# The second MLP of a two-layer encoder: the norm's scale and bias, applied to x at one place or in eight parts

## The chip, the core and the metric

The kernel runs on one core of one Trainium2 chip. The metric is the device time of one execution in microseconds (us): 1342.46 us before the change. The engines are PE (TensorE, matmuls; PEld are its weight loads), DVE (VectorE), ACT (ScalarE), POOL (GpSimd) and SP (SyncE, which issues most DMAs). Each runs its own list of instructions in order and waits for others through semaphores.

## What is computed

A trunk of two layers, 512 tokens of 1024 float32 features. Each layer is a token mixer (gated DeltaNet in layer 0, gated linear attention, GLA, in layer 1) and a squared-ReLU MLP, and each of these ends in a residual sum and a LayerNorm:

```python
x = _layernorm(DEEPNORM_ALPHA * x + m, ln1_g[i], ln1_b[i])           # m: the mixer
a = jax.nn.relu(jnp.matmul(x, mlp_w1[i]))                            # 1024 -> 4096
x = _layernorm(DEEPNORM_ALPHA * x + jnp.matmul(a * a, mlp_w2[i]),    # 4096 -> 1024
               ln2_g[i], ln2_b[i])
```

The change lies between the second `ln1` and the second MLP.

## The kernel before

**x twice.** After the GLA mixer, x exists in two forms. The transposed form, `xth` and `xtl` (a rounded high part and the rest), is what the first matmul of the MLP reads; its scale and bias were applied while it was copied out of PSUM (L168). The row form, `xt[t]` for the four tiles t of 128 tokens, each in two halves of 512 columns, is what the residual needs. When the MLP starts, it has only been centred and divided by its deviation (`whiten`, L198); scale and bias still have to be applied to it. `affine` (L200) does this: a multiplication by g (L203) and an addition of b (L204) for each half, DVE instructions on 128x512 float32. Over four tiles these are sixteen instructions, eight of each kind. g and b are broadcast to 128 partitions by four DMAs (`load_ln`, L225) into two tiles of `ln_tile`.

**The MLP.** `mlp` (L333) has 32 blocks of 128 features, in four groups of eight. The first group is computed plainly: four blocks in `proj_halves`, then f = 4 to 7 one by one in `feature`. The other three groups are computed by a seven-product scheme of the Strassen kind: `pairs` makes two blocks at a time from products 1, 2, 5, 6, 7, 3, 4 (in this order) of sums of weight halves and of sums of x. The sums of x are made once, by `combos` (L389), a generator that is advanced step by step while f = 3 to 7 run; each operand is a pair, high (ACT, L398) and low (DVE, L399). Of these, operand 3 is the last of `t_pair(2)`, and operand 7 is written over a part of x after feature 7. The second matmul uses the same scheme over 512-wide products, in `seconds`: 21 products m = 0 to 20 of four units u each, every unit six matmuls; results are added to `xt` by `adds` (L534 the first time, L536 after that).

**Order.** The loop at L758 alternates one step of `pairs` with one unit of `seconds`; in this text, product 3 means the first pair's unless another is named. All matrix products are split: high x high, high x low, low x high (`mm3`, L114), so each operand needs a cast on ACT and a subtraction on DVE (`split`, L88). Before anything runs, the framework fixes each engine's order: among the instructions that its own model of time holds ready, it takes the one that was traced first, except those marked urgent, which go ahead. Three orders are prescribed: PE's and POOL's from L723 on, and ACT's inside the loop (L757), as traced. DVE's isn't prescribed. DVE therefore takes later-traced work whenever it expects nothing earlier to be ready.

**Memory.** A tile with a tag shares its slots with others of that tag, and a new one waits until every instruction that reads or writes the old one is done, those traced later too. Two lines matter:

```python
tiles = [pool.tile([P, 2, 512], F32, name=f"ln{i}", tag=f"t{4 + i}", bufs=1) for i in range(2)]
return tuple(pool.tile([P, HF, HT], F32R, name=f"t{2 * i + j}", tag=f"t{2 * i + j}", bufs=1) for j in range(2))
```

The first is `ln_tile` (L539): g lies in tag t4, b in t5. The second is `t_pair` (L384): `t_pair(2)`, operand 3, has the tags t4 and t5 too, with one slot each.

In `combos` before, the four calls of `affine` stand between operand 6 and the sum for operand 3. Traced, they come with f = 4 (t = 0), f = 5 (t = 1, 2) and f = 6 (t = 3).

Of the kernel before, what the change touches and what calls it, by code (L numbers as in the profile page):

```python
# [13 lines left out]
ALU = mybir.AluOpType  # L14
# [7 lines left out]
NT = S // P  # L22
# [6 lines left out]
class Ctx:  # L29
# [167 lines left out]
        for q in range(2):  # L197
            nc.scalar.activation(xs[q], xs[q], AF.Identity, scale=rstd[:, 0:1], bias=nmr[:, 0:1])  # L198

    def affine(self, t, par):  # L200

        for q, x in enumerate(self.xh(t)):
            self.nc.vector.tensor_tensor(x, x, par[q], ALU.mult)  # L203
            self.nc.vector.tensor_tensor(x, x, par[2 + q], ALU.add)  # L204

    def rsqrt(self, out, x, n, scale, eps):

# [125 lines left out]
def mlp(c, w1, w2, g, b, left, before=None, out=None):  # L333
# [13 lines left out]
    with c.banks(pj=2, X=2, Y=2, Z=2), tc.tile_pool(name="mlp", bufs=2) as pool:  # L347
        acts, par, lnp = [], [], []
# [34 lines left out]
        def t_pair(i):  # L383
            return tuple(pool.tile([P, HF, HT], F32R, name=f"t{2 * i + j}", tag=f"t{2 * i + j}", bufs=1) for j in range(2))  # L384

        def x_block(i, j):
            return tuple(t[:, HF * j:HF * j + HF, HT * i:HT * i + HT] for t in (c.xth, c.xtl))

        def combos():  # L389

            f = lambda t: t.bitcast(F32)
            tmp = pool.tile([P, 2, HF, HT], F32, name="tx", tag="h", bufs=3)
            u, v = tmp[:, 0], tmp[:, 1]
            a12, a21, a22 = x_block(0, 1), x_block(1, 0), x_block(1, 1)
            op = {1: x_block(0, 0), 2: a12, 4: a22}

            def pair_of(i, src, dst):
                A.copy(dst[0], src)  # L398
                V.tensor_tensor(dst[1], src, f(dst[0]), ALU.subtract)  # L399
                op[i] = dst  # L400

            def diff(out, a, b):
                V.tensor_tensor(out, f(a[0]), f(b[0]), ALU.subtract)
                V.tensor_tensor(out, out, f(a[1]), ALU.add)
                V.tensor_tensor(out, out, f(b[1]), ALU.subtract)

            def neg(out, a, b):
                V.scalar_tensor_tensor(out, a, -1.0, f(b[0]), ALU.mult, ALU.subtract)
                V.tensor_tensor(out, out, f(b[1]), ALU.subtract)

            diff(v, a22, a21)
            yield op
            pair_of(5, v, t_pair(0))
            yield op
            diff(u, op[1], a21)
            yield op
            neg(v, u, a22)
            yield op
            pair_of(6, v, t_pair(1))
            yield op  # L420
            if before:
                for t in range(NT):
                    c.affine(t, lnp)
                    yield op
            neg(v, v, a12)
            yield op
            pair_of(3, v, t_pair(2))
            yield op
            while not_done:
                yield op  # L430
            pair_of(7, u, a21)

        def urgent():
            return tc.high_priority()
# [91 lines left out]
        def pair(src, where="ah"):  # L526
            return c.split(src, [P, HF, HT], pool=ring(where))

        def add(t, hf, ps, op=ALU.add, cs=slice(0, 512)):
            xs = c.xh(t)[hf][:, cs]  # L530
            ps = ps[:, cs]
            if (t, hf) not in touched:
                touched.add((t, hf))
                V.scalar_tensor_tensor(xs, xs, ALPHA, ps, ALU.mult, op)  # L534
            else:
                V.tensor_tensor(xs, xs, ps, op)  # L536
# [5 lines left out]
        def quarters(h):  # L542
            return [h[j][:, :, HT * i:HT * i + HT] for i in range(2) for j in range(2)]
# [4 lines left out]
        def split_q(gi, i, q):  # L548

            parts.setdefault((gi, i), []).append(c.split(blocks[BLOCK[i] + (q,)], [P, 2, 512], pool=ring("w2")))  # L550
            if (gi, i) != (0, 1):
                sums(i, q)
            if i in (6, 7, 3, 4):
                load_part(gi + 1, *BLOCK[i], q)

        def sums(i, q):

            for x, y in PLUS.get(i, ()):
                a, b = blocks[x + (q,)], blocks[y + (q,)]
                if i == 5:  # L560
                    V.tensor_tensor(a, a, b, ALU.add)
                else:
                    nc.gpsimd.dma_start(a, b, accum_op=ALU.add)  # L563

        def seconds(hs, tail):

            seq = [(gi, i) for gi in range(G - 1) for i in (1, 2, 5, 6, 7, 3, 4)]
            left = {}

            def operand(gi, i):  # L570
                a11, a12, a21, a22 = quarters(hs[gi])
                if i == 5:
                    V.tensor_tensor(a11, a11, a21, ALU.subtract)
                    V.tensor_tensor(a21, a22, a21, ALU.subtract)
                if i == 6:
                    V.scalar_tensor_tensor(a21, a11, -1.0, a22, ALU.mult, ALU.subtract)
                    V.scalar_tensor_tensor(a12, a12, -1.0, a21, ALU.mult, ALU.subtract)
                left[gi, i] = pair({1: a11, 2: a12, 5: a21, 6: a21, 7: a11, 3: a12, 4: a22}[i])

            def banks(tag):  # L580
                return [c.bank([P, 512], F32, name="p" + tag, tag=tag) for _ in range(2)]

            def adds(i, j, ps):
                if i in (1, 2):
                    add(j, 0, ps)
                elif i in (5, 7):
                    add(2 + j, 1, ps, ALU.subtract)
                else:
                    add(j, 1, ps, ALU.subtract) if i in (6, 3) else add(2 + j, 0, ps)

            for q in range(2):
                split_q(0, 1, q)
            operand(0, 1)
            yield
            due = []
            for m, (gi, i) in enumerate(seq):
                nx = seq[m + 1] if m + 1 < len(seq) else None
                if i == 1:
                    X, Y = banks("X"), banks("Y")
                Z = None if m == 0 else Z  # L600
                if m == 1:
                    Z = banks("Z")
                bk = {2: Z, 5: Y, 3: Y}.get(i) or X
                for u in range(4):
                    q, j = divmod(u, 2)
                    wh, wl = parts[gi, i][q]
                    ah, al = left[gi, i]
                    sl = slice(j * P, (j + 1) * P)
                    for k in (2 * q, 2 * q + 1):
                        c.mm3(bk[j], ah[:, k, sl], al[:, k, sl], wh[:, k % 2, :], wl[:, k % 2, :],  # L610
                              (i in (1, 5) or m == 1) and k == 0, k == HF - 1, skip_group_check=True)
                    with urgent():
                        for d in due:
                            adds(*d)
                    due = [(i, j, bk[j])] if q and (i != 2 or gi == G - 2) else []
                    if i in (6, 4) and u == 2:
                        with urgent():
                            adds(*due.pop())
                    if m == 0 and u < 2:
                        sums(1, u)  # L620
                    if nx:
                        if u in (0, 2):
                            split_q(*nx, u // 2)
                        elif u == 1:
                            operand(*nx)
                    if m >= len(seq) - 2:
                        next(tail, None)
                    yield
            for d in due:
                adds(*d)  # L630
# [92 lines left out]
        with c.in_order(mybir.EngineType.PE), c.in_order(mybir.EngineType.Pool):  # L723
            hs = {0: h}
            tail = last(G - 1, hs)
            units = seconds(hs, tail)
            halves = c.proj_halves(specs, between)
            for f, ps in enumerate(halves):
                done = act(ps, h[0][:, f, :])
                load_part(0, 0, f // 2, f % 2, done if f > 1 else None)  # L730
                if f == 0 and before:
                    lnp.extend(c.load_ln(*before, ln_tile(), acts[0]))
                    c.cols = None
            combo = combos()
            def run(n):
                for _ in range(n):
                    next(combo, None)
            op = next(combo)
# [1051 lines left out]
```

## Time and profile before

| | |
|---|---|
| time, median of 3 runs | 1342.46 us (1341.44 to 1342.73) |
| span of the profiled execution, first to last instruction | 1340.6 us |
| second MLP's loop of `pairs` and `seconds`, about | 1051 to 1290 us of the span |
| `affine`, first and last start | 1032.3 and 1045.9 us |

The execution that was profiled has no time of its own beside its span; the median is 1.9 us longer, which is what lies around the first and the last instruction. In the timeline's rows, the first number is the start in us from the span's start, the second the duration; then engine, line, operation, output<-inputs, shape and count. Instructions of one engine overlap a little: the next one starts before the one ahead has ended, so a step from start to start says what an instruction costs its engine. A bracket at the end of a row gives the idle time ahead of it and who ended it. In the table of windows, the columns are busy us and counts of PE, PEld, DVE, ACT and POOL, then the granted PE clock (1.00 is full), the DMA share and GB/s.

### The profile page before, as it was taken

How to read it: one execution, taken by the hardware profiler on the slowest of the kernel's cores; microseconds unless marked ns; L12 is line 12 of the kernel's file. 1: busy time of each engine (PE TensorE's matmuls, PEld its weight loads, DVE VectorE, ACT ScalarE, POOL GpSimd, SP SyncE). 2: the span in 40 equal slices, each digit the busy share in tenths (PEclk: the TensorE clock that was granted, in tenths of full speed). 3: DMA queues.
4: the chain of work that ended last, by engine and by line, in shares of the span. 5: the costliest groups of instructions: out<-in, count | busy, mean ns of one | idle time of the engine just before them, and what ended most of it. 6: DMA issues, size and time to landing. Idle time of an engine off the chain costs nothing.

```text
span 1340.6 us, 22226 instructions
## 1 busy us (share of the span) xinstructions
PE 1324.5 (99%) x8802; PEld 1141.1 (85%) x8802; DVE 1103.2 (82%) x1738; ACT 757.4 (56%) x1445; POOL 98.9 (7%) x160
## 2 busy tenths in 40 slices
PE   9999999999999999999999999999999999999997
PEld 7778887888888899999998988888889899999986
DVE  6798898998768888988977687977777998889885
ACT  4766657666534656656663354654467566566640
POOL 6700000000001000101001000000000000001000
PEclk9999999999999999999999999999999999999999
DMA  6321111211133665556430422222225766556411
GB/s 179 80 64 49 48 48 48 64 46 46 53 112 109 197 133 157 125 159 166 118 95 32 122 85 63 64 64 64 84 74 146 185 171 145 126 165 132 142 65 48
DMA packets 152248, 136.47 MB, mean 102 GB/s; under 512 B 9025, under 2 KB 123745, under 8 KB 152144
## 3 DMA queue, kind: packets, MB, share of 16 engines
q1 hardware_dynamic: 145280, 111.62, 28.3%
q0 software_dynamic: 6720, 23.16, 8.9%
q8 instruction: 69, 1.13, 0.4%
q14 instruction: 35, 0.29, 0.1%
q10 hardware_dynamic: 144, 0.26, 0.1%
HBM read 114.06 MB, written 2.10 MB: 87 GB/s over the span
## 4 chain that ended last, share of the span: by engine, by line
PE 86%; DVE 6%; ACT 5%; issue 1%; DMA 1%; DVEq 0%; ACTq 0%
PE pq L120 6%; PE pq L119 6%; PE pq L117 6%; PE pX L119 3%; PE pX L120 3%; PE pX L117 3%; PE pjv L117 3%; PE pjv L120 3%; PE pjv L119 3%; PE pl L119 2%; PE pl L117 2%; PE pl L120 2%; PE scp L1015 2%; PE op L1720 2%; PE lv L1583 2%; PE pY L119 2%
## 5 line engine op out<-in xcount | busy, mean ns | idle before, releaser
L98 ACT CAST wh<-wst 128x1024 fp32r<-128x1024 f32 (+1 forms) x179 | 177.4, 994 | 158.0 <-DVE wst L448 52.8
L99 DVE TENSOR_TENSOR wl<-wst,wh 128x1024 fp32r<-128x1024 f32 (+1 forms) x179 | 205.6, 1151 | 43.5 <-ACT wh L98 43.1
L99 DVE TENSOR_TENSOR w2l<-w2r,w2h 128x1024 fp32r<-128x1024 f32 x84 | 102.5, 1220 | 23.1 <-ACT w2h L98 23.1
L120 PE MATMUL pq<-xth,wl 128*128 128x256 f32 x384 | 108.6, 283 | 0.0
L117 PE MATMUL pq<-xth,wh 128*128 128x256 f32 x384 | 108.5, 283 | 0.0
L119 PE MATMUL pq<-xtl,wh 128*128 128x256 f32 x384 | 108.5, 283 | 0.0
L98 ACT CAST w2h<-w2r 128x1024 fp32r<-128x1024 f32 x84 | 88.1, 1049 | 4.6 <-DMA w2r<-in_mlp_w 2.2
L120 PE MATMUL pq<-t,wl 128*128 128x256 f32 x288 | 81.4, 282 | 0.6 <-DVE wl L99 0.6
L117 PE MATMUL pq<-t,wh 128*128 128x256 f32 x288 | 81.0, 281 | 0.1
L119 PE MATMUL pq<-t,wh 128*128 128x256 f32 x288 | 81.1, 281 | 0.0
L119 PEld LDWEIGHTS pq<-xtl,wh 128*128 128x128 f32 x384 | 73.4, 191 | 3.0
L117 PEld LDWEIGHTS pq<-xth,wh 128*128 128x128 f32 x384 | 73.3, 191 | 2.9
L119 PE MATMUL pX<-w2l,ah 128*128 128x512 f32 x192 | 75.5, 393 | 0.0
L120 PE MATMUL pX<-w2h,al 128*128 128x512 f32 x192 | 75.4, 393 | 0.0
L117 PE MATMUL pX<-w2h,ah 128*128 128x512 f32 x192 | 75.1, 391 | 0.0
L120 PEld LDWEIGHTS pq<-xth,wl 128*128 128x128 f32 x384 | 73.4, 191 | 0.0
L448 DVE TENSOR_TENSOR wst<-wst 128x512 f32<-128x512 f32 x96 | 65.0, 685 | 9.1 <-DMA wst<-in_mlp_w 8.7
L563 POOL DMA_DIRECT2D w2r<-w2r x36 | 30.9, 875 | 404.7 <-DVE w2l L99 192.1
L117 PEld LDWEIGHTS pq<-t,wh 128*128 128x128 f32 x288 | 54.4, 189 | 1.4 <-DVE h L495 0.5
L119 PEld LDWEIGHTS pq<-t,wh 128*128 128x128 f32 x288 | 54.3, 188 | 1.0
L120 PEld LDWEIGHTS pq<-t,wl 128*128 128x128 f32 x288 | 54.3, 188 | 1.0 <-DVE wl L99 1.0
L117 PE MATMUL pjv<-wh,xth 128*128 128x512 f32 x128 | 54.7, 427 | 0.0
(526 smaller groups left out, 4009.2 us busy)
## 6 DMA issues: line engine op xcount, KB each, us to landing
wst<-in_mlp_w SPq DMA_DIRECT2D x64, 512.0 KB, 4.8
w2r<-in_mlp_w SPq DMA_DIRECT2D x64, 512.0 KB, 4.1
w2r<-w2r POOLq DMA_DIRECT2D x36, 512.0 KB, 5.7
wst<-in_a_w_in SPq DMA_DIRECT2D x32, 512.0 KB, 4.1
wst<-in_b_w_in SPq DMA_DIRECT2D x32, 256.0 KB, 3.0
wst<-in_a_w_out SPq DMA_DIRECT2D x8, 512.0 KB, 3.7
wst<-in_b_w_in SPq DMA_DIRECT2D x8, 512.0 KB, 3.9
wst<-in_b_w_out SPq DMA_DIRECT2D x8, 512.0 KB, 3.7
```

The costliest lines, as they stand in the source:

```text
L98: nc.scalar.copy(hi, src)
L99: self.low = nc.vector.tensor_tensor(lo, src, hi.bitcast(F32), ALU.subtract)
L117: mm(ps, ah, bh, start=start, stop=False, **kw)
L119: mm(ps, ah, bl, start=False, stop=False, **kw)
L120: mm(ps, al, bh, start=False, stop=stop, **kw)
L448: V.tensor_tensor(a, a, b, ALU.add)
L563: nc.gpsimd.dma_start(a, b, accum_op=ALU.add)
L1015: T.matmul(ps[:, n, :], kh[:, sl], qh[:, sl], start=True, stop=True)
L1583: T.matmul(ps[:, u, :, :], lhs[:, u, :], cols(rhs, u, s, i), start=True, stop=True)
L1720: T.matmul(op[:, n, :], l, r, start=i == 0, stop=i == len(mm) - 1)
```

## The change

`affine` takes one half q of a tile instead of both. `combos` no longer calls it, so that its next steps (the sum for operand 3 and its pair) are traced two features earlier. `seconds` calls it at the first two units of the products m = 0, 1, 2 and 4, for two tiles and one half each, which is eight calls: m = 0 for half 0 of tiles 0 and 1, m = 1 for half 1 of tiles 2 and 3, m = 2 for half 1 of tiles 0 and 1, m = 4 for half 0 of tiles 2 and 3. The first additions to these halves come with the products m = 0, 2, 3 and 6. Number, shape and operands of the sixteen DVE instructions stay the same, and so do all DMAs, tiles and tags.

```diff
-    def affine(self, t, par):
-
-        for q, x in enumerate(self.xh(t)):
-            self.nc.vector.tensor_tensor(x, x, par[q], ALU.mult)
-            self.nc.vector.tensor_tensor(x, x, par[2 + q], ALU.add)
+    def affine(self, t, q, par):
+
+        x = self.xh(t)[q]
+        self.nc.vector.tensor_tensor(x, x, par[q], ALU.mult)
+        self.nc.vector.tensor_tensor(x, x, par[2 + q], ALU.add)
...
             pair_of(6, v, t_pair(1))
             yield op
-            if before:
-                for t in range(NT):
-                    c.affine(t, lnp)
-                    yield op
             neg(v, v, a12)
             yield op
             pair_of(3, v, t_pair(2))
...
             due = []
+            fresh = {0: (0, 0), 1: (2, 1), 2: (0, 1), 4: (2, 0)} if before else {}
             for m, (gi, i) in enumerate(seq):
...
                             adds(*due.pop())
+                    if m in fresh and u < 2:
+                        t, hf = fresh[m]
+                        c.affine(t + u, hf, lnp)
                     if m == 0 and u < 2:
                         sums(1, u)
```

## The prediction, made before the changed kernel was seen

> **What bounds the kernel now.** I read the page first, then the table of windows over the second MLP, then the chain that ended last between 1027 and 1080 us, and at last the timelines of PE, DVE, ACT and SP there.
>
> ```profile
> span 1340.6 us, 22226 instructions
> PE 1324.5 (99%) x8802; PEld 1141.1 (85%) x8802; DVE 1103.2 (82%) x1738; ACT 757.4 (56%) x1445; POOL 98.9 (7%) x160
> ```
> ```profile
> 1030.00:1050.00 20.00, 20.00 (x90) 16.56 (x89) 20.00 (x27) 9.28 (x12) 2.62 (x3) 1.00 0.91 246
> 1050.00:1070.00 20.00, 19.54 (x125) 17.32 (x125) 18.89 (x23) 10.74 (x15) 0.85 (x1) 1.00 0.76 175
> 1070.00:1090.00 20.00, 19.80 (x127) 17.84 (x126) 19.49 (x23) 12.59 (x20) 1.70 (x2) 1.00 0.59 132
> 1110.00:1310.00 200.00, 200.00 (x1236) 179.47 (x1235) 171.02 (x209) 118.04 (x168) 12.45 (x16) 1.00 0.50 129
> ```
>
> PE is the bound: from 1110 to 1310 it is never idle, and DVE's 15% of slack there (171.02 of 200) is worth nothing. The one stretch in which DVE sets the pace is 1030 to 1090: it is busy for all 20 us of the first window, and PE loses a little in the two that follow. The chain of waits runs over DVE there:
>
> ```profile
> 1030.05 1.22 DVE wl L99
> ...
> 1061.37 6.32 DMA wst<-in_mlp_w
> ...
> 1078.03 1.15 DVE wl L99
> ...
> 1079.22 0.39 PE pq L120
> ```
>
> How much PE loses shows in its timeline, by the steps between starts (0.23 us for a 512-wide matmul, 0.12 for a 256-wide one).
>
> ```profile
> 1056.37 0.39 PE L120 MATMUL pX<-w2h,al 128*128 128x512 f32 x1
> 1056.86 0.39 PE L117 MATMUL pq<-t,wh 128*128 128x256 f32 x1
> 1057.08 0.28 PE L119 MATMUL pq<-t,wh 128*128 128x256 f32 x1
> ...
> 1058.49 0.28 PE L119 MATMUL pq<-t,wh 128*128 128x256 f32 x1
> 1059.13 0.38 PE L120 MATMUL pq<-t,wl 128*128 128x256 f32 x1 [0.36 <-DVE wl L99]
> ...
> 1078.74 0.28 PE L119 MATMUL pq<-t,wh 128*128 128x256 f32 x1
> 1079.22 0.39 PE L120 MATMUL pq<-t,wl 128*128 128x256 f32 x1 [0.20 <-DVE wl L99]
> ```
>
> At product 5 of the first pair PE is 0.26 us late, and its next step takes 0.22 for 0.12; at product 6 a step takes 0.64 for 0.12: 0.26 + 0.10 + 0.52 = 0.88 us, the first stall. The second, at product 6 of the second pair, is 0.48 for 0.12 and a slow step behind it: 0.46 us. Together 1.34 us, and no edit of DVE's order in this stage can win more.
>
> **The change part by part.** Sixteen DVE instructions move; none is added and none removed.
>
> ```profile
> L203 DVE TENSOR_TENSOR xt<-xt,ln x8: 684/686/690, 1032.3 to 1044.7; 128x512 f32<-128x512 f32 x8
> ```
> ```profile
> L204 DVE TENSOR_TENSOR xt<-xt,ln x8: 683/687/689, 1034.1 to 1045.9; 128x512 f32<-128x512 f32 x8
> ```
> ```profile
> 1045.30 1.29 DVE L204 TENSOR_TENSOR xt<-xt,ln 128x512 f32<-128x512 f32 x2
> 1046.50 1.22 DVE L99 TENSOR_TENSOR al<-h,ah 128x1024 fp32r<-128x1024 f32 x1
> 1047.64 1.22 DVE L99 TENSOR_TENSOR wl<-wst,wh 128x1024 fp32r<-128x1024 f32 x1
> ```
>
> Each lasts 0.69 us and costs DVE 0.60 (two in 1.20); a 1024-wide one costs 1.14 (1046.50 to 1047.64). So 16 x 0.60 = 9.7 us of DVE time is taken out of 1032 to 1046, where it stands ahead of work that PE needs.
>
> It can't go where the new calls stand, though. g and b lie in the only slots of t4 and t5, and operand 3 gets the same two slots. Its high half can't be written until all eight multiplications are done, its low half not until all eight additions are, whichever product they were traced with. Product 3 of the first pair needs both. So the sixteen instructions become fillers: taken wherever the planner sees DVE without better-ranked work, and all due before product 3.
>
> When is operand 3 ready then? DVE's work is conserved, so I count it.
>
> ```profile
> 1031.18 1.22 DVE L408 SCALAR_TENSOR_TENSOR tx<-tx,xth 128x1024 f32<-128x1024 f32 x1
> ...
> 1054.65 1.22 DVE L399 TENSOR_TENSOR t<-tx,t 128x1024 fp32r<-128x1024 f32 x1
> ...
> 1062.99 1.22 DVE L99 TENSOR_TENSOR w2l<-w2r,w2h 128x1024 fp32r<-128x1024 f32 x1
> ...
> 1067.78 0.69 DVE L448 TENSOR_TENSOR wst<-wst 128x512 f32<-128x512 f32 x1 [1.11 <-DMA wst<-in_mlp_w]
> 1068.39 1.22 DVE L574 TENSOR_TENSOR h<-h 128x1024 f32<-128x1024 f32 x1
> ...
> 1071.33 1.22 DVE L99 TENSOR_TENSOR w2l<-w2r,w2h 128x1024 fp32r<-128x1024 f32 x1
> ```
> ```profile
> 1064.71 0.28 PE L119 MATMUL pq<-t,wh 128*128 128x256 f32 x1
> ```
>
> Before, operand 3's low half is made at 1054.65, ten us ahead of product 3, whose second matmul, the first to read it, is at 1064.71. DVE shows no idle time between 1030 and 1062.99. After the change, all that it did up to 1062.99 still comes ahead of that half, since it is ranked better (splits of weights, sums, the first addition to x) or has to precede it (the sixteen). One more instruction slips in, L574, which waits for nothing and is traced with m = 1, ahead of the last eight: +1.14. With no idle time the half would be done at 1064.13.
>
> There will be idle time, since the cover goes. Ahead of the split of feature 7's weights stand now, from 1031.18, only five 1024-wide instructions (L408, L409, feature 6's split, the split of h, operand 6) and one filler: 5 x 1.14 + 0.60 = 6.3, to 1037.5.
>
> ```profile
> 1035.13 0.59 ACT L359 ACTIVATE h<-pj 128x512 f32<-128x512 f32 x1
> 1038.54 1.05 ACT L98 CAST wh<-wst 128x1024 fp32r<-128x1024 f32 x1 [2.82 <-DMA wst<-in_mlp_w]
> 1039.49 0.63 ACT L360 ACTIVATE h<-h 128x512 f32<-128x512 f32 x1
> 1041.96 1.05 ACT L98 CAST wh<-wst 128x1024 fp32r<-128x1024 f32 x1 [1.83 <-DMA wst<-in_mlp_w]
> ```
>
> The cast of these weights waits 2.82 us for its DMA and ends at 1039.59. It stands in ACT's list right behind feature 4's first activation (1035.13) and ahead of its second, which shows that the planner takes the weights to have landed by then. So it will place their DVE split early as well, ahead of most fillers, and on the chip DVE stands there with the fillers queued behind it: 1039.59 - 1037.5 = 2.1 us. In the trace of before the sixteen hid this wait. Bounds: 0, if the planner puts enough fillers ahead, and 5.0, if also the next load's 1.83 and the 1.11 that DVE waited for a load at 1067.78 come on top. I take 2.1, the wait whose place the rows show.
>
> Operand 3 is then done at 1064.13 + 2.1 = 1066.2, and the matmul of 1064.71 runs at some 1066.3, **1.6 us later** than before. The first stall is inside this number: PE may wait at product 5 (L495, which frees its bank, stands in the same late list) or only at product 3, and the later of the two counts. The second stall should go: L574 is done already, so that DVE's lag there is 2.1 - 1.14 = 1.0, less than PE's 1.6. That is -0.46. Nothing after 1090 changes, for PE is the bound and the additions to x find their operands ready. No DMA is moved; SP's and POOL's lists keep their order.
>
> Sum: +1.6 - 0.46 = +1.1. On the profiled span 1340.6 + 1.1 = 1341.7; the median lies 1.9 above the span, so 1343.6 us, 0.09% up.
>
> What does a wait cost PE beyond its length? The rows show the end of the kernel, where PE has stopped (window, PE busy, clock, DMA share, GB/s):
>
> ```profile
> 1332.00:1333.00 1.00, 0.93 (x8) 1.00 0.00 0
> ...
> 1337.00:1338.00 1.00, 0.00 (x0) 0.80 0.49 184
> 1338.00:1339.00 1.00, 0.00 (x0) 0.50 0.91 340
> ```
>
> The granted clock falls to half some 4.7 us after the last matmul. The forecast's waits are shorter (1.6 + 0.88 = 2.5 in all), so they add nothing.
>
> **The rivals.** *The cover holds.* No idle time opens; operand 3 is done at 1064.1 and read at 1064.2 against 1064.71, so PE is 0.5 earlier there and the second stall goes as well: -1.0, 1341.5 us. For it speaks that DVE had no hole before; against it ACT's row at 1038.54.
>
> *More waits for loads.* All 5.0 us reach DVE: operand 3 at 1069.1, +4.5 - 0.46 = +4.0, 1346.5 us. It decides from about 3.6 us of idle time on. For it speaks the DMA share of 0.91 between 1030 and 1050; against it that fillers stand between the loads. The Trainium skill ("TensorE: Matmul & The Clock Gate", Part 1) lets the clock fall to half after one idle window of about 3.4 us, sooner than the 4.7 of the rows; by that rule this rival, were its wait in one piece, would also run the next window at half pace, an estimate of 1.7 us more (1348.2).
>
> *The last fillers starve* (slower). If the next product's splits, its two weight sums and its operands could also go ahead of the eight lowest-ranked instructions, product 3 would wait for them.
>
> ```profile
> 1068.58 0.62 ACT L98 CAST wh<-wst 128x512 fp32r<-128x512 f32 x1 [5.71 <-DVE wst L448]
> 1069.11 1.04 ACT L98 CAST w2h<-w2r 128x1024 fp32r<-128x1024 f32 x1
> ```
>
> Five of them (w2l, L561, al, L576, L577 from 1071.33 on) are 5 x 1.14 = 5.7: operand 3 at 1071.9, +7.3 - 0.46. PE would be idle for over 4.7 us and return at half clock; with the 5 us at half pace that the kernel's start shows (below), +2.5. That is +9.3, 1351.8 us. Against it: their casts come behind the one of 1068.58 in ACT's prescribed order, whose slot is free only after product 3. It decides from the point where that cast gets another slot.
>
> ```profile
> 1.53 3.17 PE L775 MATMUL idle<-pz 128*128 128x512 f16 x7 [1.53 <-DVE pz L1303]
> ...
> 6.52 0.38 PE L775 MATMUL idle<-pz 128*128 128x512 f16 x1
> ```
>
> (Seven in about 2.96 us, 0.42 each, against 0.23 at full pace.)
>
> *The change does what it says*, each part beside its product: ruled out by the shared slots, since g and b would be overwritten.
>
> **How the numbers follow.** Forecast, between -0.3 and +3: 0.52. Cover holds: 0.26. More waits: 0.12. Starved fillers: 0.10. A measurement of this kernel can tell about 0.2%, 2.7 us, from no change. Faster than that is beyond the 1.34 us that can be won: 0.02 for what I don't see. Slower: the last two, 0.22. Within: 0.76. The range takes in the whole 1.34 that can be won and the second rival with some room (+4.7): 1341.0 to 1347.2; the starved case and the edges stay out, 0.15.
>
> **What would show it.** Right: L203 and L204 spread over 1031 to 1064 with all sixteen ahead of operand 3's L399, which moves from 1054.65 to about 1065; DVE idle ahead of a wl near 1037, ended by ACT; PE waiting at product 5 or 3; no stall near 1079. Wrong: multiplications after product 3 has run (the slots aren't shared as I read them), no idle time on DVE near 1037, or PE idle for more than 4 us with a clock below 1.00.

## The result, and the profile after

The changed kernel takes 1348.49 us (median; 1348.31 to 1349.42) against 1342.46 before: a ratio of 1.0049, 95% interval 1.0038 to 1.006, so some 6.0 us slower. The prediction said 1343.6, with a range up to 1347.2.

In the code after the change all lines behind `combos` stand four lower (L495 before is L491 after, L491 is L487, L448 is L444, L573 and L574 are L569 and L570). The page's head and the windows that answer to those of before:

```profile
span 1347.3 us, 22229 instructions
...
PE 1326.4 (98%) x8802; PEld 1143.3 (85%) x8802; DVE 1104.0 (82%) x1738; ACT 757.8 (56%) x1445; POOL 98.8 (7%) x160
```
```profile
1030.00:1050.00 20.00, 20.00 (x90) 16.57 (x89) 18.40 (x23) 9.66 (x13) 2.62 (x3) 1.00 0.94 268
1050.00:1070.00 20.00, 14.65 (x76) 13.12 (x75) 16.79 (x20) 8.97 (x12) 0.85 (x1) 0.83 0.65 154
1070.00:1090.00 20.00, 20.00 (x129) 18.14 (x128) 19.30 (x24) 12.21 (x18) 1.70 (x2) 1.00 0.37 68
1110.00:1310.00 200.00, 200.00 (x1252) 180.16 (x1251) 174.49 (x215) 120.99 (x173) 12.44 (x16) 1.00 0.51 131
```

Everything is lost in one window, 1050 to 1070: PE is busy for 14.65 us where it was busy for 19.54, and in part of it the clock is below full. In 1070 to 1090 PE has become better (20.00 for 19.80), and later nothing differs. DVE isn't busier in the bad window; it is idle for 3.2 us of it.

The timeline of the changed kernel, all engines, shows the place. The first and the last row are PE's last matmul ahead of product 5 and product 5's first; between them stands what the bracket leads back to, step by step.

```profile
1056.24 0.39 PE L120 MATMUL pX<-w2h,al 128*128 128x512 f32 x1
...
1057.99 0.69 DVE L203 TENSOR_TENSOR xt<-xt,ln 128x512 f32<-128x512 f32 x1
1058.71 1.04 ACT L398 CAST t<-tx 128x1024 fp32r<-128x1024 f32 x1 [6.41 <-DVE xt L203]
1058.72 0.69 DVE L204 TENSOR_TENSOR xt<-xt,ln 128x512 f32<-128x512 f32 x1
1059.79 1.22 DVE L399 TENSOR_TENSOR t<-tx,t 128x1024 fp32r<-128x1024 f32 x1 [0.38 <-ACT t L398]
1061.10 0.37 ACT L487 COPY h<-pq 128x256 f32<-128x256 f32 x1 [1.34 <-DVE t L399]
...
1061.51 0.42 DVE L491 TENSOR_TENSOR h<-h,pq 128x256 f32<-128x256 f32 x1 [0.49 <-ACT h L487]
...
1061.98 0.58 PE L117 MATMUL pq<-t,wh 128*128 128x256 f32 x1 [5.35 <-DVE h L491]
```

Read backwards: product 5 waits for L491, the addition that frees its bank. L491 waits for L487, ACT's copy of product 1 into the new `h`. L487 waits for L399, the low half of operand 3, and L399 waits for the cast of its high half, which waits for the last multiplication by g. That operand 3 comes behind all sixteen was foreseen. That the *copy of product 1* waits for operand 3 was not. These are the two tiles that tie them (`new_h`, L378, and `combos`, L392):

```python
return [pool.tile([P, HF, S], F32, name="h", tag="h", bufs=3) for _ in range(2)]
tmp = pool.tile([P, 2, HF, HT], F32, name="tx", tag="h", bufs=3)   
```

`tmp` holds u and v, from which the operands are made, and has the third slot of tag h; `hs[0]` has the other two. The `h` into which product 1 is copied takes `tmp`'s slot, so it comes free when operand 3's low half, its last reader, is done. The same rows in the kernel before:

```profile
1055.96 0.37 ACT L491 COPY h<-pq 128x256 f32<-128x256 f32 x1 [2.22 <-DVE t L399]
...
1056.39 0.41 DVE L495 TENSOR_TENSOR h<-h,pq 128x256 f32<-128x256 f32 x1
...
1056.85 0.19 PEld L117 LDWEIGHTS pq<-t,wh 128*128 128x128 f32 x1 [0.52 <-DVE h L495]
```

The chain was there before, and already without slack: the copy waited 2.22 us for operand 3 and ended at 1056.33, the addition ran at 1056.39, and PE's first 0.26 us were lost behind it. Operand 3's low half moved from 1054.65 to 1059.79 (+5.14), and product 5 from 1056.86 to 1061.98 (+5.12): every microsecond came through.

Behind the wait PE runs at half clock for a while (table of windows, the column before the last two):

```profile
1060.00:1061.00 1.00, 0.00 (x0) 0.00 (x0) 1.00 (x1) 0.00 (x0) 0.00 (x0) 0.92 1.06 201
1061.00:1062.00 1.00, 0.02 (x1) 0.02 (x1) 0.44 (x2) 0.90 (x2) 0.00 (x0) 0.50 0.69 127
1062.00:1067.00 5.00, 5.00 (x23) 5.00 (x24) 4.55 (x4) 3.53 (x5) 0.00 (x0) 0.50 0.38 103
1067.00:1068.00 1.00, 1.00 (x6) 0.87 (x5) 0.09 (x1) 0.49 (x2) 0.00 (x0) 0.67 0.55 134
1068.00:1069.00 1.00, 1.00 (x6) 0.82 (x5) 0.14 (x1) 1.00 (x2) 0.00 (x0) 1.00 1.05 315
```

0.92 means half clock for the last 0.16 us of that window, from 1060.84 on; 0.67 means half clock up to 1067.66. From 1061.98 PE has work, so it loses half of 5.68 us, 2.84. The sum on the spans: +5.12 + 2.84, less the 1.08 of the old stalls that are gone (0.10 + 0.52 + 0.46; the 0.26 is already in the 5.12) = +6.9; the spans differ by 1347.3 - 1340.6 = 6.7, the medians by 6.0.

### The profile page after: what moved, and what is told of

Same layout as the page of the kernel before. It is cut to its first block, busy times and chain, and to the rows that moved or that the text cites. A ratio compares the mean times of both kernels' runs of the same rounds, so it can differ in the third digit from the quotient of the medians.

```text
span 1347.3 us, 22229 instructions
## 1 busy us (share of the span) xinstructions
PE 1326.4 (98%) x8802; PEld 1143.3 (85%) x8802; DVE 1104.0 (82%) x1738; ACT 757.8 (56%) x1445; POOL 98.8 (7%) x160
## 4 chain that ended last, share of the span: by engine, by line
PE 88%; ACT 5%; DVE 4%; issue 2%; DMA 1%; POOL 0%; DVEq 0%; SPq 0%; POOLq 0%; ACTq 0%
PE pq L117 6%; PE pq L120 6%; PE pq L119 6%; PE pX L119 3%; PE pX L117 3%; PE pX L120 3%; PE pjv L117 3%; PE pjv L120 3%; PE pjv L119 3%; PE pl L119 2%; PE pl L117 2%; PE pl L120 2%; PE scp L1015 2%; PE op L1720 2%; PE lv L1583 2%
## 5 line engine op out<-in xcount | busy, mean ns | idle before, releaser
L444 DVE TENSOR_TENSOR wst<-wst 128x512 f32<-128x512 f32 x96 | 64.9, 685 | 9.2 <-DMA wst<-in_mlp_w 8.8
L99 DVE TENSOR_TENSOR al<-h,ah 128x1024 fp32r<-128x1024 f32 x42 | 51.2, 1220 | 4.9 <-ACT ah L98 4.9
```

The lines of the kernel that those rows point to most:

```text
L99: self.low = nc.vector.tensor_tensor(lo, src, hi.bitcast(F32), ALU.subtract)
```

## The experiments

My theory: two shared slots in a row (t4 and t5, then h) make the sixteen due before product 5, and the half clock is charged on top. The main rival: DVE simply has the sixteen queued ahead of L491, whichever slots there are. In the windows tables below, the columns are those of the ones above.

**1. `tmp` apart.** In the second MLP, u and v leave tag h and take one slot each of the tags al and ah, which `seconds` uses for its operands. This breaks the second link; it puts a weaker tie in its place, since a later operand of `seconds` may now have to wait for u or v (the cast of the next one did, 1.10 us at 1060.84, without holding PE up).

```diff
-            tmp = pool.tile([P, 2, HF, HT], F32, name="tx", tag="h", bufs=3)
-            u, v = tmp[:, 0], tmp[:, 1]
+            tmp = None if before else pool.tile([P, 2, HF, HT], F32, name="tx", tag="h", bufs=3)
+            u, v = [pool.tile([P, HF, HT], F32, name="tx", tag=s, bufs=2) for s in ("al", "ah")] if before else (tmp[:, 0], tmp[:, 1])
```

> The changed kernel, but in the second MLP the two sums of x that feed the operands (u and v, one tile with the third slot of tag h) get two tiles in slots of their own kind (tags al and ah); scale and bias stay where the change puts them, and operand 3 still shares t4 and t5 with g and b. Theory (two shared slots in a row): product 1's copy then no longer waits for operand 3, so the sixteen are due before product 3 only, as forecast: PE idle ahead of product 5 under 1.5 us (5.4 in the changed kernel), granted clock 1.00, 1341.5 to 1344.5 us. Rival (DVE simply has the sixteen queued ahead of the addition that frees product 5's bank): the wait stays over 4 us, 1347 to 1349.5 us.

Measured: 1341.16 us (1340.41 to 1343.83) against 1342.24 before, ratio 0.9994 (0.9985 to 1.0003): the whole loss is gone, and the median lies 0.3 us under the range that was expected. The window, then the timelines of PE (product 5's first matmul), ACT and DVE in this kernel:

```profile
1050.00:1070.00 20.00, 20.00 (x126) 18.01 (x126) 19.82 (x27) 11.36 (x16) 0.85 (x1) 1.00 0.77 173
```
```profile
1059.53 0.28 PE L117 MATMUL pq<-t,wh 128*128 128x256 f32 x1
```
```profile
1055.53 0.37 ACT L487 COPY h<-pq 128x256 f32<-128x256 f32 x1 [0.17 <-PE pq L120]
1055.84 1.05 ACT L398 CAST t<-tx 128x1024 fp32r<-128x1024 f32 x1
```
```profile
1057.47 0.41 DVE L491 TENSOR_TENSOR h<-h,pq 128x256 f32<-128x256 f32 x1
...
1059.54 1.21 DVE L399 TENSOR_TENSOR t<-tx,t 128x1024 fp32r<-128x1024 f32 x1
```

PE doesn't wait at all: product 5 starts at 1059.53, before operand 3's low half is begun (1059.54). The copy now waits for product 1 itself and stands ahead of the cast of operand 3, and L491 runs in time although fifteen of the sixteen have run ahead of it and only one comes behind. So DVE's load did not hold PE up, and the rival falls; the tie between operand 3 and the copy of product 1 did. Had product 5 still followed that half by 0.97 us, as in the changed kernel (1061.01 to 1061.98), it would have started 2.2 us later here (an estimate). Two limits: the edit takes away both the wait for the slot and the copy's place behind the cast on ACT, where it could not have run before about 1059.7 in the changed kernel, and their shares aren't measured apart; and the times can't be compared as they stand with the changed kernel's, since the whole stage lies later in this execution.

This profiled execution took 1343.83 us, 2.7 over the median, for a reason outside the stage, which shows in its own windows:

```profile
40.00:60.00 20.00, 19.84 (x88) 16.25 (x88) 11.70 (x28) 14.36 (x33) 11.93 (x25) 0.91 0.30 79
```

Half clock for 3.6 of these 20 us (9% lost) costs 1.8 of the 2.7 us; in the kernel before, this window had 1.00. All times of the stage stand some 2.9 us later here: PE's last matmul ahead of product 5 starts at 1059.30, for 1056.37 before the change. So 1059.54 answers to about 1056.6 there: operand 3's low half is some 2 us later than before the change, not 5.14 as in the changed kernel. That a half as late as the changed kernel's or the forecast's costs nothing without the tie is not shown.

**2. Other operands for scale and bias.** The sixteen instructions stay, but read `xth` in place of g and b, which breaks the first link only.

```diff
-                        c.affine(t + u, hf, lnp)
+                        c.affine(t + u, hf, [c.xth[:, HF + k, :].bitcast(F32) for k in range(4)])
```

> The changed kernel, but the sixteen instructions read four resident blocks of xth in place of g and b, so scale and bias are other numbers; count, shape and place in the code are the same, and g and b are loaded but not read. Theory: operand 3 no longer has to wait for them, its low half is made before 1052 us (1059.79 in the changed kernel), several multiplications stand behind product 5, PE idle there under 1 us, clock 1.00, 1341 to 1343 us. Rival (the sixteen cost DVE the same time in the same stage, whatever slot they read): 1346 us or more.

Measured: 1342.16 us (1340.96 to 1343.66), ratio 1.0001 (0.9992 to 1.001). The window, then the groups of the operands' low halves and of the multiplications (ns, first and last start):

```profile
1050.00:1070.00 20.00, 19.97 (x126) 17.65 (x126) 20.00 (x28) 10.79 (x16) 0.85 (x1) 1.00 0.75 184
```
```profile
L399 DVE TENSOR_TENSOR t<-tx,t x6: 1216/1224/1226, 446.8 to 1047.7; 128x1024 fp32r<-128x1024 f32 x6
```

```profile
L203 DVE TENSOR_TENSOR xt<-xt,xth x8: 682/688/692, 1021.9 to 1064.4; 128x512 f32<-128x512 f32 x8
```

Operand 3 is made at 1047.7, at least twelve microseconds earlier (PE's stage lies 2.4 us later in this execution), and multiplications run up to 1064.4, behind product 5's start at 1058.86. DVE is busy for all 20 us and PE isn't held up: the same work in the same stage costs nothing once operand 3 need not wait for it. Each of the two edits takes the loss away alone, so both links had to be there for it.

**3. The parts at the old place.** The kernel before, with `affine` called for one half at a time.

```diff
-                    c.affine(t, lnp)
+                    for q in range(2):
+                        c.affine(t, q, lnp)
```

> The kernel before with affine cut in parts as after the change (one half of a tile per call), all eight calls at the old place. Theory: the cut itself costs nothing, 1342.0 to 1343.0 us. Rival (the cut, not the place, makes the difference): 1346 us or more.

Measured: 1342.37 us (1341.74 to 1342.72), ratio 1.0 (0.9991 to 1.0009). The cut costs nothing; the place does.

**4. The kernel before with `tmp` apart**, by the edit of experiment 1.

> The kernel before, with u and v in tiles of their own as in the first of these runs. Theory: in the kernel before, product 1's copy waited 2.22 us for operand 3 too; with that wait gone the 0.26 us at product 5 and the slow step behind it go, 1341.5 to 1342.6 us. Rival (DVE's backlog sets that stall): 1342.3 to 1343.2 us, the stall still there.

Measured: 1342.38 us (1341.69 to 1344.97), ratio 1.0002 (0.9993 to 1.0011). Its windows and the one wait of PE that is left:

```profile
1050.00:1070.00 20.00, 20.00 (x128) 17.91 (x127) 19.49 (x24) 12.60 (x18) 0.85 (x1) 1.00 0.69 148
1070.00:1090.00 20.00, 19.65 (x127) 17.62 (x126) 17.96 (x21) 11.84 (x18) 1.70 (x2) 1.00 0.59 132
```
```profile
1079.05 0.38 PE L120 MATMUL pq<-t,wl 128*128 128x256 f32 x1 [0.35 <-DVE wl L99]
```

The first stall is gone, as the theory says (20.00 for 19.54), and the second is still there, 0.35 us. The time can't tell: 1342.38 lies in both expectations. The window supports the chain, but weakly: DVE's order changed too, and operand 3's low half starts at 1052.66 here, 2 us earlier than in the kernel before.

**5. PE kept busy.** The changed kernel with matmuls into an unused bank ahead of product 5.

```diff
+                if before and n == 0:
+                    dz = c.bank([P, S], F32, name="dz", tag="Z")
+                    for _ in range(22):
+                        T.matmul(dz, c.xth[:, HF, :P], c.xth[:, HF, :], start=True, stop=True)
                 Y = bank()
                 prod(5, Y, True)
```

> The changed kernel with 22 further 512-wide matmuls on PE ahead of the first pair's product 5, into a bank that nothing reads: 22 x 0.23 = 5.0 us, which fill the wait. Theory (the wait costs twice, once by its length and once by the half clock behind it, which the changed kernel shows from 1060.8 to 1067.7, 5.7 us at half pace from 1061.98 on, 2.8 us lost): the wait's end stays near 1062, clock 1.00 throughout, 1345.2 to 1346.5 us. Rival (after the wait DVE's splits set the pace, whatever the clock): 1347.8 to 1349 us.

Measured: 1346.82 us (1346.6 to 1348.99), ratio 1.0035 (1.0022 to 1.0047). PE's timeline and the window behind the wait:

```profile
1062.11 0.39 PE L117 MATMUL pq<-t,wh 128*128 128x256 f32 x1 [0.55 <-DVE h L491]
```
```profile
1062.00:1067.00 5.00, 4.89 (x33) 4.54 (x34) 4.47 (x5) 5.00 (x8) 0.00 (x0) 1.00 0.34 97
```

Product 5 starts where it did (1062.11), the clock is full, and PE gets 33 matmuls into the five microseconds that held 23. The median is 1.7 us below the changed kernel's, the profiled spans differ by 2.4 (1347.3 - 1344.9), the rows gave 2.84: the half clock is worth 1.7 to 2.8 us, and the rival falls. One of the five executions took 1348.99, with a mean granted clock of 0.997 against 0.998 to 0.999 in the others; it has no trace. My range was missed by 0.3 us, since it took the 2.84 off the median, while the changed kernel's profiled execution lies 0.46 us above its median.

**6. A shorter idle time.** The same with 7 in place of 22.

> The same with 7 of these matmuls, 1.6 us: PE is then idle for some 3.9 us in place of 5.4. Theory (the clock falls 4.2 to 4.7 us after the last matmul, as in the two places where the traces show it): it doesn't fall, clock 1.00, 1345.2 to 1346.5 us. Rival (one idle window of 3.4 us is enough): half clock behind the wait, 1347.5 to 1349 us.

Measured: 1348.99 us (1347.74 to 1349.49), ratio 1.0046 (1.0033 to 1.0059). PE's timeline and the windows:

```profile
1056.30 1.78 PE L501 MATMUL dz<-xth 128*128 128x512 f32 x7
1062.31 0.51 PE L117 MATMUL pq<-t,wh 128*128 128x256 f32 x1 [4.23 <-DVE h L491]
```
```profile
1062.00:1063.00 1.00, 0.69 (x3) 0.69 (x4) 0.47 (x2) 1.00 (x2) 0.00 (x0) 0.71 0.02 0
1063.00:1065.00 2.00, 2.00 (x12) 2.00 (x11) 2.00 (x2) 2.00 (x3) 0.00 (x0) 0.50 0.00 0
1065.00:1066.00 1.00, 1.00 (x7) 1.00 (x7) 1.00 (x2) 0.86 (x2) 0.00 (x0) 0.58 0.46 116
```

My theory of the clock fell here. PE was idle for 4.23 us, came back at 1062.31, and at 1062.42 (0.71: half for 0.58 us) the clock fell all the same. It was full again at 1065.84 (0.58: half for 0.84 us), after 3.42 us.

**7. Eight of the sixteen left out**: `fresh = {0: (0, 0), 1: (2, 1)}`.

> The changed kernel without the calls of the products m = 2 and m = 4: four of the eight halves of x get neither scale nor bias, and eight DVE instructions, 4.8 us, are left out. Theory (what stands ahead of operand 3 sets the wait, and PE has some slack before it): operand 3's low half some 4.8 us or more before 1059.79, PE idle at product 5 under 1 us, clock 1.00, 1341.0 to 1342.6 us, so more than the half of the loss goes. Rival (a price in proportion to the moved instructions): half of the 6.0 us, 1344.8 to 1346 us.

Measured: 1341.73 us (1340.51 to 1342.53), ratio 0.9995 (0.9986 to 1.0004). DVE's timeline and the window:

```profile
1052.56 1.22 DVE L399 TENSOR_TENSOR t<-tx,t 128x1024 fp32r<-128x1024 f32 x1
```
```profile
1050.00:1070.00 20.00, 20.00 (x129) 18.17 (x128) 18.77 (x23) 12.23 (x17) 0.85 (x1) 1.00 0.65 130
```

Operand 3 is made 7.2 us earlier than in the changed kernel, 4.8 for the eight instructions and the rest for L569 and L570, which now come behind it. With that the chain has slack, and all of the loss is gone, not half. The price isn't per instruction; it sets in where operand 3 comes later than product 5 allows.

**8. All sixteen left out**: `fresh = {}`.

> The changed kernel without any call of affine in the second MLP: x gets neither scale nor bias there, and all sixteen instructions are left out. It gives the floor that this stage has: both stalls of the kernel before, 1.34 us, should be gone and nothing else, 1340.8 to 1341.8 us. If it were below 1340.5, the sixteen would cost something outside this stage too.

Measured: 1341.65 us (1341.21 to 1341.98), ratio 0.9993 (0.9984 to 1.0002). This is the floor of the stage: within the noise it is no lower than experiment 1 or 7, so no cost of the sixteen instructions shows where they stand well.

**9. Idle for some 3 us.** Experiment 5 with 12 matmuls, after experiment 6 had shown that a clock rule of mine was wrong.

> The changed kernel with 12 further 512-wide matmuls ahead of product 5, 2.7 us: PE is then idle for some 3.1 us (4.23 with 7 of them, where the clock still fell, for 3.4 us). Theory of the clock formed on these traces (it is judged in steps of about 3.4 us, since it was at half for 6.8 us in the changed kernel and for 3.4 with 7 matmuls, and an idle time shorter than one step can't fill one): it stays at 1.00, 1346.2 to 1347.2 us, as with 22 matmuls. Rival (any idle time of some 3 us lowers it): half clock behind the wait for 3.4 us, 1.7 us lost, 1347.8 to 1349.2 us.

Measured: median 1348.6 us, ratio 1.0043 (1.0029 to 1.0056), but in two groups: 1346.31 and 1346.48, and 1348.6, 1348.79 and 1348.93. The profiled execution is the one of 1346.48; its PE timeline and the window behind the wait:

```profile
1062.01 0.38 PE L117 MATMUL pq<-t,wh 128*128 128x256 f32 x1 [2.64 <-DVE h L491]
```
```profile
1062.00:1068.00 6.00, 5.99 (x38) 5.46 (x39) 5.51 (x6) 5.74 (x8) 0.00 (x0) 1.00 0.38 103
```

In it the clock stayed full, as the theory said; the other group lies at the rival's time, with a mean granted clock over the span of 0.996 to 0.997 against 0.998 to 0.999. So the run doesn't decide. The dearer executions lost clock somewhere, but no trace of one was taken, and the place isn't shown: executions 2 to 3 us longer with a mean clock of 0.997 also came where PE has no such wait (two of 21 of the kernel before, 1344.45 and 1344.71; experiment 1's 1343.83, which lost it between 40 and 60 us) and once in experiment 5. Three of five is more than in any of these, which speaks for this place without proving it.

## Why the prediction was wrong

**What bounds the kernel, and the most that can be won: in line with the runs.** PE's two stalls are the 1.34 us that can be won in this stage. The three kernels without either loss (experiments 1, 7 and 8) came to 1341.16, 1341.73 and 1341.65, 0.7 to 1.1 us below the kernel before in their comparisons, though none of the three is clear of noise.

**Sixteen instructions that can't stand at their new calls: right.** All sixteen run ahead of operand 3's low half:

```profile
L203 DVE TENSOR_TENSOR xt<-xt,ln x8: 684/686/689, 1035.6 to 1058.0; 128x512 f32<-128x512 f32 x8
```
```profile
L204 DVE TENSOR_TENSOR xt<-xt,ln x8: 684/686/692, 1041.3 to 1058.7; 128x512 f32<-128x512 f32 x8
```

Experiment 2 shows that it is the slot of g and b that holds operand 3 back.

**"All due before product 3": this is the step that failed.** They were due before product 5. The prediction looked for who else uses the slots of g and b, and stopped there; it did not ask the same of the slot from which operand 3 is made. It even named L495 at product 5 as a place where PE might wait, but took that for a place in DVE's list and priced it at product 3. Experiment 1 shows that with this one tie gone sixteen fillers ahead of an operand 3 that is 2 us late cost nothing. In the terms of its sum: the +1.6 at product 3's second matmul was +7.08, from 1064.71 to 1071.79, made up of 5.12 ahead of product 5 and 2.84 by the half clock, less the 0.62 of the first stall that was gone (together 7.34, 0.3 more than the row shows); the -0.46 came as forecast.

```profile
1071.79 0.28 PE L119 MATMUL pq<-t,wh 128*128 128x256 f32 x1
```

The evidence stood in the trace of before: ACT's row at 1055.96, in which the copy of product 1 waits 2.22 us for L399, and the 0.26 us behind it, which the prediction quoted as a stall and did not follow back.

**When operand 3 is ready: wrong, it came five microseconds earlier.** The forecast had its low half done at 1066.2; it was done at 1061.0. What it counted ahead of that half, the splits for the next products and the first addition to x, came behind it, since these wait for product 5 or stand behind the held copy in ACT's prescribed order. From 1054.65 the half moved to 1059.79 by L569 and L570, which slipped ahead (2 x 1.14), one more weight sum (0.60), and DVE's waits of 1.48 and 0.38, 4.7 of the 5.14 us. DVE's timeline shows the largest of them:

```profile
1039.00 1.22 DVE L99 TENSOR_TENSOR wl<-wst,wh 128x1024 fp32r<-128x1024 f32 x1 [1.48 <-ACT wh L98]
...
1052.11 1.22 DVE L569 TENSOR_TENSOR h<-h 128x1024 f32<-128x1024 f32 x1
...
1053.85 1.22 DVE L570 TENSOR_TENSOR h<-h 128x1024 f32<-128x1024 f32 x1
```

**DVE idle at feature 7's weights: right in kind and place**, 1.48 us for the 2.1 forecast.

**The second stall goes: right** (20.00 of 20 between 1070 and 1090).

**No half clock: wrong as a consequence.** The price of a wait beyond its length was seen and set aside, because the forecast's waits were short. One of the signs named there for a wrong forecast, PE idle for more than 4 us with the clock below 1.00, is what came.

**The rivals.** "The last fillers starve" had the right outcome, PE idle for over 4.7 us and back at half clock, at the wrong product and by another mechanism. Its 1351.8 us were 3.3 too many. "More waits for loads" did not come: DVE's waits ahead of operand 3 sum to 1.9 us, not 5.0, so that the 1348.2 us which stand beside it are near the measured 1348.49 by luck. None of the rivals contained the slot of `tmp`.

## What to carry to other kernels

When work is tied to a tile by a shared slot, follow the slots on: who takes the slot that the held-up instruction itself releases, and who waits for that, until PE is reached. The trace of before shows the way: a bracket leads from product 5's weights to the addition, another from the copy to operand 3, and between them stands the addition's own operand. A stall that is there already marks a chain without slack, so find out what ends it before pricing a delay on it as small. And count a wait of PE of four microseconds or more as its length plus some two more: with 5.35 and 4.23 us of idle time the clock fell to half in these runs.

## What the hardware showed beyond that

The clock behind a wait goes in steps. In the changed kernel it was at half for 6.82 us (1060.84 to 1067.66), with 7 added matmuls for 3.42 (1062.42 to 1065.84): two steps and one of about 3.4 us. It fell 4.2 and 4.3 us after the last matmul had ended, in the second case 0.1 us after PE had started again, so the prediction's 4.7 us from the kernel's end is a delay and no limit under which a wait is free. The Trainium skill ("TensorE: Matmul & The Clock Gate", Part 1) has a free-running window of about 3.4 us after which the clock changes: the steps agree with it. Whether a wait as short as the 2.64 us of experiment 9 can cost a step, no trace here shows.
